# The MLP's seven half-block products over the prompt's tokens only, with the sample's tokens on the stationary side

## The chip, the cores and the metric

The kernel runs on one core of one Trainium2 chip. The metric is the device time of one execution in microseconds; lower is better. A profiled execution has its own time, and a span from its first to its last instruction. TensorE appears as PE (matmuls) and PEld (loads of the stationary side), VectorE as DVE, ScalarE as ACT, GpSimd as POOL and SyncE as SP. SP and POOL here mostly issue DMAs.

## The reference

The model has two layers over 1024 tokens of a prompt and 8 × 16 = 128 tokens of a sample, with 1024 features, all in fp32. Only the MLP of each layer is changed:

```python
def sq_relu_mlp(h, w_up, w_down):
    return jnp.square(jax.nn.relu(h @ w_up)) @ w_down
...
xp = xp + sq_relu_mlp(rmsnorm(xp, norm_ffn[layer]), w_up[layer], w_down[layer])
xs = xs + sq_relu_mlp(rmsnorm(xs, norm_ffn[layer]), w_up[layer], w_down[layer])
```

`w_up` is 1024 × 4096 and `w_down` 4096 × 1024, so a layer's MLP has 32 chunks of 128 hidden rows (`NF`). After layer 1 a final RMSNorm gives the outputs for both kinds of token.

## The kernel before, in words

Features lie on the 128 partitions and the tokens are columns: 1152 of them (`T`), the sample's 128 last. A matrix product keeps fp32 precision by splitting each operand into a high and a low fp32r part, and runs three matmuls, hi·hi, hi·lo and lo·hi (`SPLIT`). In a matmul the weights are stationary (128 × 128) and the tokens move (128 × n columns).

`rest(layer, ...)` does the second half of a layer: the output projection, the MLP, and the start of what follows. Its MLP uses a seven-product scheme on 2 × 2 blocks, in place of eight. The blocks of the tokens are two halves of the features by two halves of the 1152 columns (`TW` = 576 each). A product over 576 columns is two matmuls of 288 (`TQ`).

**Up.** As the output projection's chunks arrive, `evac` adds them to the residual, and `combine(c)` forms the seven combinations of the normed tokens (`b11`, `t2`, `t1`, `b21`, `t3`, `b22`, `t4`), each split into hi and lo; eleven steps for each of four feature chunks c. A unit `unit(m)` (16 a layer) then makes two chunks of hidden rows. `raw(m)` loads its weights, `two_sums` and `seven(i)` form and split the seven weight combinations, two products ahead of their use, into six buffers that take turns. `mms` (line 1525) runs the 12 matmuls of a product for one column quarter, and `take`/`done` sum the products from PSUM, apply the token's RMSNorm factor, ReLU (L1532) and square (L1533), and form the combinations that the down product needs. POOL's queue writes these to DRAM (`hb_d`). The first unit begins with the feature chunks 0 to 2 of its first three products, while `combine(3)` still runs, and then does chunk 3.

**Down.** `todos` lists 7 products × 16 items (`j`, two chunks of hidden rows each); in layer 1 the last product, 5, runs its column halves `n` one after the other. For an item, SP loads the tokens' combination (`load_b`) and the weights (`load_w`, `resident`); ACT and DVE split them (`split_b`, `weights_hi` L1693, `weights_lo` L1699), two to three items ahead; `products` (L1750) runs 12 matmuls for each column quarter. `run_at(i)` holds what is issued ahead of item i. The first two of these, `begin(0)` and `begin(1)`, are issued inside the last unit, before its products 5 and 6. When a chain of products ends, DVE adds the PSUM banks to the residual (L1755), and small steps of the next stage (`later`) are put between items: squares, splits for layer 1, the final norm's outputs (L1914).

The work on one engine runs in the order in which it stands in that engine's program. A scheduler may move an instruction ahead of others by its estimate of when it is ready, except the ones issued by `pinned`. An instruction that waits holds up all that stand behind it on its engine.

Of the kernel before, what the change touches and what calls it, by code (L numbers as in the profile page):

```python
# [15 lines left out]
P = 128  # L16
# [17 lines left out]
TW = T // 2  # L34
TQ = T // 4
TF = 96
# [88 lines left out]
def tile_trunk(ctx, tc, ins, outs):  # L125
# [54 lines left out]
    hb_d = [dram.tile([7, NF // 2, P, TW], F32, name=f"hb_d{l}") for l in range(2)]  # L180
# [76 lines left out]
    def rstd_of(r, pl, acc, scale, eps, name, pin=lambda ins: ins, tp=P):  # L257

        ms = bank(f"ms_{name}")
        for j in range(NG):
            ins = mm(ms[:tp, j:j + 1], acc[:, j * tp:(j + 1) * tp], ones[:, 0:1], start=True, stop=True)
            if j == 0:
                pin(ins)
        v = pl.tile([P, 2, NG], F32, tag="rv", name=f"v_{name}")
        m, y = v[:tp, 0], v[:tp, 1]
        nc.vector.tensor_scalar(m, ms[:tp, 0:NG], scale, eps, ALU.mult, ALU.add)
# [9 lines left out]
        def diag(dg):  # L278
            box["dg"] = dg[:tp, :NG * tp]
            for j in range(NG):  # L280
                nc.vector.tensor_scalar_mul(dg[:tp, j * tp:(j + 1) * tp], ident[:tp, :tp], y[:, j:j + 1])

        def rows():
            ps = bank(f"rr_{name}")
            pin(mm(ps[:, :NG * tp], ones[:tp], box["dg"], start=True, stop=True))
            ACT(r, ps[:, :NG * tp], AF.Copy)
# [1053 lines left out]
    def rest(layer, ks, cat, rst, mp, then, soon=None):  # L1340
# [17 lines left out]
        spare = [own(f"xr{n}", F32) for n in range(4)]  # L1358
        few = [own(f"hl{n}", F32R, 1024) for n in range(2)]
        third = own("th", F32R)  # L1360
        temps = [own(f"tm{n}", F32) for n in range(2)]
# [9 lines left out]
        combos = {k: pair(slots[n], T) for n, k in enumerate(there)}  # L1371
        combos.update({(key, 2): pair(low[n], T) for n, key in enumerate(("t1", "b21", "t3"))})

        def combo(key, c):

            if (key, c) not in combos:
                combos[key, c] = pair(place(*where[key, c], F32R, f"{key}{name}"), T)
            return combos[key, c]
# [22 lines left out]
        def combine(c):  # L1401
# [3 lines left out]
            one, two = slice(0, TW), slice(TW, T)  # L1405
            d, t3, t2, t4 = (t[:, h] for t in temps for h in (one, two))

            def halves(key, src, w):
                hi, lo = (combo(key, c)[:, i] for i in range(2))
                if w is None:  # L1410
                    split(hi, lo, src)
                else:
# [13 lines left out]
                    lambda: halves("t4", t4, None)]  # L1426

        def evac(n, ps, g):
# [4 lines left out]
            if g == NG - 1:  # L1433
                put(xr_d[layer][fc], x[fc])
                if n % 2:
                    todo.extend(combine(fc - 4))

                    todo.append((lambda: (old(n + 3), old(n + 4))) if n < 4 else (lambda: raw(n // 2 - 2)))
            some(3)
            if n == KC - 1 and g == 1:  # L1440
                seven(0)


        raws, ups, parts = {}, {}, [0]
        pinned = tc.keep_in_program_order

        def raw(m):

            if m < NF // 2 and m not in raws:
                raws[m] = [spare[m % 2 * 2 + e][:, :1024] for e in range(2)]  # L1450
                for e in range(2):
                    dma(raws[m][e], ins["w_up"][layer, 2 * m + e])

        def two_sums(m, pin=lambda ins: ins):
            a11, a21, a22 = raws[m][0][:, :512], raws[m][1][:, :512], raws[m][1][:, 512:]
            s1 = ups["s1"] = sp.tile([P, 512], F32, "st", f"s1{name}{m}")
# [4 lines left out]
        def seven(i):  # L1461

            if i in ups or i >= 7 * NF // 2:
                return
            m, k = divmod(i, 7)
            a1, a2 = raws[m]
            a11, a12, a21, a22 = a1[:, :512], a1[:, 512:], a2[:, :512], a2[:, 512:]
            if k == 0:
                src = a11
            elif k == 1:  # L1470
                if "s1" not in ups:
                    two_sums(m)
                src = a11
            elif k == 2:
                src = ups.pop("s1")
# [11 lines left out]
            if k == 0 and m:  # L1487
                pinned(ACT(w[:, 0], src, AF.Copy))
                pinned(tt(w[:, 1], src, f(w[:, 0]), ALU.subtract))
            else:  # L1490
                split(w[:, 0], w[:, 1], src)
            ups[i] = w

        works = [("b11", 0), ("t2", 1), ("t1", 2), ("b21", 0), ("t3", 1), ("b22", 2), ("t4", 1)]
        hids = []
        tmps = [temps[n // 4][:, n % 4 * TQ:n % 4 * TQ + TQ] for n in range(8)]

        t3, t2 = extra[:, :TW], extra[:, TW:]

        def last_sum(m):  # L1500

            pinned(tt(t3, hids[m % 2 * 2 + 1][:, :TW], t2, ALU.subtract))
            put(hb_d[layer][6, m], t3)

        def unit(m):

            if m:
                raw(m + 1)
            if m == 0:
                hids.extend([own("th", F32), *(place(c, i, F32, f"hd{name}") for c, i in ((5, 1), (6, 0), (6, 1)))])  # L1510
            hd = [hids[m % 2 * 2 + e] for e in range(2)]
            banks, tmp = {}, {}

            def to(e, half, n):

                return hd[e][:, half * TW + n * TQ:half * TW + n * TQ + TQ]

            def mms(k, n, ks):
                key, b = works[k]
                if (b, n) not in banks:  # L1520
                    banks[b, n] = bank(f"u{name}{m}{b}{n}")
                w = ups[7 * m + k]
                for c in ks:
                    for i, (a, h) in enumerate(SPLIT):
# [506 lines left out]
```

## Time and profile before

| what | value |
|---|---|
| median of 3 runs | 2714.48 us (2708.94 to 2715.2) |
| time of the profiled execution | 2718.14 us |
| its span | 2716.3 us |
| mean granted TensorE clock | 0.993 of full speed |
| DVE / ACT busy | 2039.7 / 1364.3 us |
| MLP of layer 0: up, down | 580.8 to 946.7 us, 946.7 to 1307.1 us |
| MLP of layer 1: up, down | 1975.4 to 2342.4 us, 2342.4 to about 2704.7 us |

The profiled execution's time is 1.8 us over its span. The two MLPs, four stretches of some 360 us, take a little over half of the span. A matmul's duration in a trace includes its way through the array, so the cost of one in a stream is read from the distance between starts. In a timeline row stand the start, the duration of the whole run of equal instructions, the engine, the line, the operation, output<-inputs, the shape and the count; a bracket gives the idle time before and what ended it. Idle time of DVE, ACT or a queue costs nothing unless PE waits for it.

### The profile page before, as it was taken

To read this page: it belongs to the slowest core of one execution; us is meant where nothing else is said; L and a number is where in the kernel's file an instruction comes from. 1 tells how busy PE (TensorE), PEld (TensorE's weight loads), DVE (VectorE), ACT (ScalarE), POOL (GpSimd) and SP (SyncE) were. 2 spreads that over 40 slices of the span, in tenths; PEclk is the share of its full clock that TensorE was granted. 3 is DMA by queue.
4 is the path that set the end of the run, shared out by engine and by line. 5 is a ranking of instruction groups with operands and counts; after the bars stand their busy time and mean duration, and the time that the engine had idled before them with its cause. 6 is when DMAs were issued, how large, how long until landed. Compare 5 with 4: busy or idle time off the path is not lost.

```text
span 2716.3 us, 50519 instructions
## 1 busy us (share of the span) xinstructions
PE 2661.6 (98%) x19362; PEld 2552.7 (94%) x19362; DVE 2039.7 (75%) x4105; ACT 1364.3 (50%) x2854; POOL 331.1 (12%) x599
## 2 busy tenths in 40 slices
PE   8999999999999999999999999999999999999998
PEld 8888877899999999999999999988999999999998
DVE  8999986887777755768577777778787777647587
ACT  6344456755555533445355555556555555534344
POOL 1100111131111100000011111110321111100001
PEclk9999999999999999999999999999999999999999
DMA  4344547543333486335444444446533333674344
GB/s 159 109 125 149 151 152 232 173 143 139 139 139 142 150 283 228 110 108 185 142 135 136 141 138 139 134 142 226 177 136 142 143 139 148 234 259 132 97 122 146
DMA packets 173203, 422.90 MB, mean 156 GB/s; under 512 B 25968, under 2 KB 53808, under 8 KB 170912
## 3 DMA queue, kind: packets, MB, share of 16 engines
q1 hardware_dynamic: 135696, 288.38, 32.6%
q0 software_dynamic: 37120, 131.27, 14.0%
q8 instruction: 152, 2.49, 0.4%
q14 instruction: 91, 0.75, 0.1%
q10 hardware_dynamic: 144, 0.02, 0.0%
HBM read 289.60 MB, written 117.34 MB: 150 GB/s over the span
## 4 chain that ended last, share of the span: by engine, by line
PE 84%; DVE 8%; DMA 3%; ACT 3%; issue 2%; SPq 0%; POOL 0%; DVEq 0%; ACTq 0%; POOLq 0%
PE pd L1750 26%; PE um L1525 25%; PE psc L225 10%; PE psp L225 4%; PE psoa L225 2%; PE avc L486 2%; PE tpc L474 2%; PE f L225 1%; PE ava L415 1%; PE zs L587 1%; DVE y L754 1%; PE zc L1261 1%; PE so L621 1%; PE psg L225 1%; PE psa L225 1%
## 5 line engine op out<-in xcount | busy, mean ns | idle before, releaser
L225 PE MATMUL psc<-h,hl_wc 128*128 128x384 f32 x1728 | 329.4, 340 | 0.0
L225 PEld LDWEIGHTS psc<-h,hl_wc 128*128 128x128 f32 x1728 | 297.3, 188 | 9.2 <-issue 7.9
L1525 PE MATMUL um<-sl,hl_m 128*128 128x288 f32 x1548 | 240.5, 296 | 0.0
L1525 PEld LDWEIGHTS um<-sl,hl_m 128*128 128x128 f32 x1548 | 218.0, 189 | 0.0
L1750 PE MATMUL pd<-tm,hl_wd 128*128 128x288 f32 x1584 | 214.7, 294 | 0.0
L1750 PEld LDWEIGHTS pd<-tm,hl_wd 128*128 128x128 f32 x1584 | 211.3, 189 | 0.0
L754 DVE SCALAR_TENSOR_TENSOR y<-u,dw,y 128x1024 f32<-128x1024 f32 (+1 forms) x232 | 177.6, 806 | 0.7
L1532 ACT ACTIVATE hdm<-hdm 128x288 f32<-128x288 f32 x192 | 84.7, 442 | 156.4 <-DVE hdm L1531 154.6
L225 PE MATMUL psp<-h,hl_wi 128*128 128x384 f32 x864 | 162.4, 340 | 0.0
L186 DVE TENSOR_TENSOR tm<-xr,tm 128x576 fp32r<-128x576 f32 (+1 forms) x120 | 85.7, 715 | 93.6 <-ACT tm L185 93.3
L225 PEld LDWEIGHTS psp<-h,hl_wi 128*128 128x128 f32 x864 | 148.3, 188 | 6.2 <-issue 5.1
L185 ACT ACTIVATE tm<-xr 128x576 fp32r<-128x576 f32 (+1 forms) x120 | 77.6, 646 | 94.8 <-PE pd L1750 76.2
L1525 PE MATMUL um<-sl,hl 128*128 128x288 f32 x756 | 119.1, 296 | 0.0
L1750 PE MATMUL pd<-th,hl_wd 128*128 128x288 f32 x792 | 113.5, 296 | 3.8 <-DVE th L186 3.6
L1750 PE MATMUL pd<-xr,hl_wd 128*128 128x288 f32 x792 | 112.6, 296 | 0.0
L1750 PEld LDWEIGHTS pd<-th,hl_wd 128*128 128x128 f32 x792 | 108.0, 190 | 4.7 <-DVE th L186 4.1
L1228 ACT ACTIVATE s<-s,mxc 128x640 f32<-128x640 f32 (+4 forms) x128 | 88.8, 694 | 40.0 <-DVE mxc L1225 38.2
L1750 PEld LDWEIGHTS pd<-xr,hl_wd 128*128 128x128 f32 x792 | 108.2, 190 | 0.0
L1525 PEld LDWEIGHTS um<-sl,hl 128*128 128x128 f32 x756 | 106.4, 188 | 0.8
L1750 PE MATMUL pd<-tm,hl 128*128 128x288 f32 x768 | 104.9, 295 | 0.0
L185 ACT ACTIVATE whc<-tpc 128x512 fp32r<-128x512 f32 (+1 forms) x144 | 72.3, 524 | 63.8 <-PE tpc L474 60.5
L1750 PEld LDWEIGHTS pd<-tm,hl 128*128 128x128 f32 x768 | 103.1, 188 | 0.0
(532 smaller groups left out, 6536.9 us busy)
## 6 DMA issues: line engine op xcount, KB each, us to landing
xr<-hb_d SPq DMA_DIRECT2D x208, 288.0 KB, 2.9
xr<-in_w_up_dram SPq DMA_DIRECT2D x64, 512.0 KB, 4.1
hb_d<-hdm POOLq DMA_DIRECT2D x96, 288.0 KB, 2.4
hb_d<-t POOLq DMA_DIRECT2D x96, 288.0 KB, 2.4
wm<-in_w_down_dram SPq DMA_DIRECT2D x64, 256.0 KB, 3.8
st_wd<-in_w_down_dram SPq DMA_DIRECT2D x64, 256.0 KB, 3.4
st_wc<-in_w_in_c_dram SPq DMA_DIRECT2D x44, 256.0 KB, 2.9
xm_d<-xo POOLq DMA_DIRECT2D x16, 576.0 KB, 3.7
```

The source lines that it names most:

```text
L185: ACT(hi, src, AF.Copy)
L186: return tt(lo, src, f(hi), ALU.subtract)
L225: mm(ps()[:, :G], hl[:, a, at:at + P], act[g][k // 4][b][:, k % 4, :], start=n == 0, stop=n == len(todo) - 1)
L415: mm(st["av"][64 * m:64 * m + 64, o0:o0 + n], vs[:, j, i], st["w"][gi][:, c0:c0 + n], start=gi == 0, stop=gi == last)
L474: nc.tensor.transpose(tp[:, c0 + q * P:c0 + (q + 1) * P], blocks.get(j, tile_q), ident)
L486: mm(st["av"][:, o0:o0 + n], vs[:, j, i].rearrange("p a d -> p (a d)"), src[:, c0:c0 + n], start=st["done"] == 0, stop=st["done"] == nmm - 1)
L587: mm(box["z"][at // 512][own, at % 512:at % 512 + kw], qb[:, own], k[:, b * kw:b * kw + kw], start=True, stop=True)
L754: stt(src if j == CW - 1 else dst, src, wj, dst, ALU.mult, ALU.add)
L1228: ACT(s[:, :n], s[:, :n], AF.Exp, bias=mx, scale=-1.0, accum_out=tot)
L1525: mm(banks[b, n][:, :TQ], w[:, a, c * P:c * P + P], combo(key, c)[:, h, n * TQ:n * TQ + TQ], start=k < 3 and c == 0 and i == 0, stop=c == ...
L1532: ACT(y, y, AF.Relu)
L1750: mm(ps, w[:, a, m * P:m * P + P], b[:, h, (n - ns[0]) * TQ:(n - ns[0]) * TQ + TQ], start=first and s == 0, stop=j == NJ - 1 and s == 2, s ...
```

## The change

- The seven products run over the prompt's 1024 tokens alone, in halves of 512 (`TH`). A product is one matmul of 512 columns where two of 288 stood; only layer 1's last product has two halves of 256.
- Two units are merged into one (`units(u)`, 8 a layer), since a product's 512 columns fill a PSUM bank. A product's weights for both (`e` = 0, 1) lie next to each other, in three pairs of buffers that take turns where there were six single ones; `seven(i, e)` still runs two products ahead. The weights of the next pair are loaded when the last use of the ones before has been split, and not a unit earlier.
- The sample's 128 tokens are left out of the seven products. They are the stationary side of four ordinary products (`s1` with weights 0 and 2, `s2` with 3, `sd` with 6), in which the same split weights move: 48 matmuls of 256 columns in a pair of units (L1616), and 192 of 512 columns in a layer's down part (L1909). `combine` gets two more steps for `s1`, `s2`, `sd`.
- The sample's hidden rows come out with tokens on the partitions. `sample_rows` applies the norm factor and ReLU at the start of the next pair, `sample_hidden` turns them with four PE transposes (L1581), squares, splits and writes them to DRAM (`hs_d`). The down part loads them (`load_s`, a further SP load for 128 of the items), and `sample_back` turns each of its three sums with four transposes and adds it to the residual.
- The first pair begins with the chunks 0 to 2 of products (0,0), (1,0), (2,0) and (0,1); the second index is `e`.
- Down takes four PSUM banks a chain, and one for the sample. `last_sum` of the last pair moves from item 3 to item 0. The final norm's last piece is 256 tokens of the prompt, and its outputs come in two blocks of 128 tokens, where there were three of 96.

```diff
-TW = T // 2
-TQ = T // 4
-TF = 96
+TH = 512
+TQ = 256
+NS = slice(TP, T)
...
+        def sample_combo(key, c):
+            return [home(k, c)[:, NS] for k in {"s1": ("b11", "t2"), "s2": ("b21", "b22"), "sd": ("t1", "t3")}[key]]
...
-                    lambda: halves("t4", t4, None)]
+                    lambda: halves("t4", t4, None),
+                    lambda: (halves("s1", x1[:, NS], w1), halves("s2", x2[:, NS], w2),
+                             ACT(sd, x1[:, NS], AF.Copy, scale=w1)),
+                    lambda: (stt(sd, x2[:, NS], w2, sd, ALU.mult, ALU.subtract), halves("sd", sd, None))]
...
-            if i % 6 < 4:
-                w = sp.tile([P, 2, 512], F32R, "hl", f"hl_{name}{i}")
-            else:
-                w = pair(few[i % 6 - 4])
...
+            if i not in ups:
+                if i % 3 < 2:
+                    both = [sp.tile([P, 2, 512], F32R, "hl", f"hl_{name}{i}{a}") for a in range(2)]
...
+                    w = [t.rearrange("p a t -> p (a t)") for t in both]
+                else:
+                    w = few
+                ups[i] = [by_unit(t) for t in w]
...
+            if k > 4:
+                raw(m + 2, k - 5)
...
+        def sample_rows(u):
...
+            ACT(f(at[0]), samples.pop(u)[:, :512], AF.Relu, scale=token_rows["s"])
...
+        def sample_hidden(u):
...
+            for n in range(4):
+                nc.tensor.transpose(tp[:, n * P:n * P + P], f(y)[:, n * P:n * P + P], ident)
...
+            ACT(y, tp[:, :512], AF.Square)
...
-                        mm(banks[b, n][:, :TQ], w[:, a, c * P:c * P + P], combo(key, c)[:, h, n * TQ:n * TQ + TQ],
+                        mm(banks[b, e], w[a][:, c], combo(key, c)[:, h],
...
+            def sample(k):
...
+                        mm(samples[u][:, e * 256:e * 256 + 256], sample_combo(key, c)[h],
+                           w[a][:, c].rearrange("p e t -> p (e t)"), start=k == 0 and c == 0 and i == 0,
...
+                early = ((0, 0), (1, 0), (2, 0), (0, 1))
...
+                if u and k == 0:
+                    last_sum(u - 1)
+                    sample_rows(u - 1)
+                if u and k == 1:
+                    sample_hidden(u - 1)
...
-        at(3, 5, last_sum, NF // 2 - 1)
+        at(0, -1, last_sum, NU - 1)
+        at(0, -1, sample_rows, NU - 1)
+        at(2, 7, sample_hidden, NU - 1)
...
+            for q, (a, h) in enumerate(SPLIT):
+                mm(rows[e], s[:, h], w[:, a], start=j == 0 and q == 0 and k != 0, stop=j == NJ - 1 and q == 2 and k != 3,
+                   skip_group_check=k in (3, 0))
```

How the instructions move shows at two places. The first is PE's program where the up part of layer 0 begins. Before, from the second product's first matmul on (`um` are PSUM banks, `t2m` and `sl`, `lo` the token combinations, `hl_m` the split weights):

```order
L1525 MATMUL um_6309<-t2m_01_5841,hl_m_6272 128x288 [waits Activation_49]
L1525 MATMUL um_6309<-t2m_01_5841,hl_m_6272 128x288
L1525 MATMUL um_6309<-t2m_01_5841,hl_m_6272 128x288 [waits DVE_49]
L1525 MATMUL um_6309<-t2m_11_5998,hl_m_6272 128x288 x3
L1525 MATMUL um_6309<-t2m_21_6145,hl_m_6272 128x288 x3
L1525 MATMUL um_6319<-t2m_01_5841,hl_m_6272 128x288 x3
L1525 MATMUL um_6319<-t2m_11_5998,hl_m_6272 128x288 x3
L1525 MATMUL um_6319<-t2m_21_6145,hl_m_6272 128x288 x3
L1525 MATMUL um_6341<-sl_5644,hl_m_6299 128x288 [waits Activation_49]
```

And now, from the third group's end on; `hl_5633` and `hl_m_6244`, `hl_m_6245` are weights:

```order
L1604 MATMUL um_6350<-sl_5645,hl_5633 128x512 [waits DVE_49]
L1604 MATMUL um_6350<-sl_5646,hl_5632 128x512 x2
L1604 MATMUL um_6350<-sl_5646,hl_5633 128x512
L1604 MATMUL um_6350<-lo_5637,hl_5632 128x512 x2
L1604 MATMUL um_6350<-lo_5637,hl_5633 128x512
L1604 MATMUL um_6368<-b11m_00_5808,hl_m_6244 128x512 [waits Activation_49]
L1604 MATMUL um_6368<-b11m_00_5808,hl_m_6244 128x512
L1604 MATMUL um_6368<-b11m_00_5808,hl_m_6245 128x512 [waits DVE_49]
```

A group is 9 matmuls of 512 columns where there were 18 of 288, and a fourth group, the first product for `e` = 1, has its own weights to wait for.

The second place is ACT's program where up ends and down begins in layer 0. Before (`hdm` are hidden rows, `th` and `xr` the first split tokens of the down part, `hl_wd` its split weights):

```order
L185 ACTIVATE hl_m_10144<-xr_5629 128x512 [waits DVE_49]
L185 ACTIVATE hl_m_10178<-xr_5630 128x512
L185 ACTIVATE th_10272<-xr_10214 128x576 [waits DMAHW1_49,DMASW7_49,DMASW3_49]
L185 ACTIVATE xr_10275<-xr_10214 128x576 [waits DMAHW2_49,DVE_49]
L1532 ACTIVATE hdm_60_6277<-hdm_60_6277 128x288 [waits DMASW4_49,DVE_49]
L1533 ACTIVATE hdm_60_6277<-hdm_60_6277 128x288 [waits Activation_49]
L1693 ACTIVATE hl_wd_10266<-lo_10219 128x512 [waits DMAHW4_49,PE_49]
L1532 ACTIVATE hdm_60_6277<-hdm_60_6277 128x288 [waits DVE_49]
```

Now (`usm` is the sample's PSUM bank, complete with the last matmul of the up part):

```order
L1628 ACTIVATE xr_5630<-xr_5630 128x512 [waits DVE_49]
L1629 ACTIVATE xr_5630<-xr_5630 128x512 [waits Activation_49]
L1573 ACTIVATE sl_9079<-usm_8770,v_m_6411 128x512 [waits PE_49]
L186 ACTIVATE th_9024<-xr_8964 128x512 [waits DMAHW1_49,DMASW0_49,DVE_49]
L1628 ACTIVATE hdm_51_6424<-hdm_51_6424 128x512 [waits DVE_49]
L1629 ACTIVATE hdm_51_6424<-hdm_51_6424 128x512 [waits Activation_49]
L1830 ACTIVATE hl_wd_9018<-lo_8968 128x512 [waits DMAHW4_49]
```

The first tokens and weights of the down part are now split behind the sample's ReLU (L1573), which waits for PE's last matmul of the up part; before, they stood four and more hidden-row steps ahead of that end.

More of the change, by code (lines that the diff above doesn't have):

```diff
@@ new lines, in seven @@
+            if i == 1:
+                hl = pair(third) if e == 0 else ups["spare"]
+                parts = [hl[:, a].rearrange("p (c t) -> p c t", c=4) for a in range(2)]
+            else:
+                parts = [w[:, :, e] for w in ups[i]]
+            src = src.rearrange("p (c t) -> p c t", c=4)
+            if k == 0 and u:
+                pinned(ACT(parts[0], src, AF.Copy))
+                pinned(tt(parts[1], src, f(parts[0]), ALU.subtract))
+            else:
+                split(parts[0], parts[1], src)
@@ L1494, in rest @@
+            ups[i, e] = parts
+            if k > 4:
+                raw(m + 2, k - 5)
         works = [("b11", 0), ("t2", 1), ("t1", 2), ("b21", 0), ("t3", 1), ("b22", 2), ("t4", 1)]
[L1495 to L1518, printed above, removed]
+        sample_works = {0: ("s1", 0), 3: ("s2", 0), 2: ("s1", 1), 6: ("sd", 1)}
@@ new lines, in rest, with hid, t2, put_pair @@
+        hids = {}
+        NU = NF // 4
+        token_rows = {}
+        samples = {}
+        def hid(e, half):
+            if (e, half) not in hids:
+                hids[e, half] = {(0, 0): lambda: own("th", F32), (1, 0): lambda: place(5, 1, F32, f"hd{name}"),
+                                 (0, 1): lambda: spare[2], (1, 1): lambda: spare[3]}[e, half]()[:, :1024]
+            return hids[e, half]
+        t3 = extra[:, :1024]
+        def t2():
+            return nx.sums[:, :1024]
+        def put_pair(k, u, src):
+            put(hb_d[layer][k, 2 * u:2 * u + 2].rearrange("m p t -> p m t"), src.rearrange("p (m t) -> p m t", m=2))
@@ new lines, in products @@
+            ps = banks[m, n][:, :b.shape[2]]
+            for s, (a, h) in enumerate(SPLIT):
+                mm(ps, w[:, a, m * P:m * P + P], b[:, h], start=first and s == 0, stop=j == NJ - 1 and s == 2,
+                   skip_group_check=k not in heads)
+            if j == NJ - 1:
+                for e, half in out[k]:
+                    at = half * TH + (n or 0) * TQ
+                    xs = x[4 * e + m][:, at:at + b.shape[2]]
+                    pinned(tt(xs, xs, ps, ALU.add))
+        rows = {}
@@ new lines, in sample_back @@
+        def sample_back(k):
+            e = sums[k][0]
+            tp = bank(f"pt{layer}{k}")
+            for m in range(4):
+                nc.tensor.transpose(tp[:, m * P:m * P + P], extra[:, 512 + m * P:512 + m * P + P], ident)
+            for m in range(4):
+                xs = x[4 * e + m][:, NS]
+                tt(xs, xs, tp[:, m * P:m * P + P], ALU.add)
+            if k != 6:
+                later.extend(then(x, e, 2, None, sq))
+        order_of = [chain_k for chain in chains for chain_k in chain]
@@ L1872, in then0 @@
             splits = [lambda c=c: n1.split(x[c][:, cols], c, cols) for c in cs]
-            if half == 0:
+            if half == 2 and e == 1:
+                return squares + splits
+            if half != 1:
                 early.extend(splits)
```

391 lines of the change are left out of this document (236 added, 155 removed).

## The prediction

> **What bounds the kernel now.** I read the page first: busy shares, then the chain that ended last, by engine and by line.
>
> ```profile
> span 2716.3 us, 50519 instructions
> PE 2661.6 (98%) x19362; PEld 2552.7 (94%) x19362; DVE 2039.7 (75%) x4105; ACT 1364.3 (50%) x2854; POOL 331.1 (12%) x599
> PE 84%; DVE 8%; DMA 3%; ACT 3%; issue 2%; SPq 0%; POOL 0%; DVEq 0%; ACTq 0%; POOLq 0%
> PE pd L1750 26%; PE um L1525 25%; PE psc L225 10%; PE psp L225 4%; PE psoa L225 2%; PE avc L486 2%; PE tpc L474 2%; PE f L225 1%; PE ava L415 1%; PE zs L587 1%; DVE y L754 1%; PE zc L1261 1%; PE so L621 1%; PE psg L225 1%; PE psa L225 1%
> ```
>
> PE is busy nearly throughout, and the two MLP lines alone make 51% of the chain. Inside the MLPs the question is whether anything else holds PE up. PE's waits in layer 0's MLP, then in layer 1's (columns: total us, times, longest):
>
> ```profile
> PE pd L1750 <- DVE th L186: 1.9, 1, 1.9
> PE um L1525 <- ACT hl_m L185: 1.2, 1, 1.2
> PE um L1525 <- DVE hl_m L186: 0.7, 1, 0.7
> ...
> PE um L1525 <- ACT hl_m L185: 1.7, 1, 1.7
> PE pd L1750 <- DVE th L186: 1.7, 1, 1.7
> ```
>
> Each of these happened once, at the up part's start (`hl_m`) or at its handover to down (`th`). Between these places PE never waits. So the change is worth what it does to PE's stream, plus what it does at these seams; DVE's and ACT's work counts only where it becomes late.
>
> **PE's stream.** Layer 0's down part in PE's timeline, its start and the first instruction behind it:
>
> ```profile
> 946.68 1.10 PE L1750 MATMUL pd<-th,hl_wd 128*128 128x288 f32 x7
> 949.70 2.65 PE L1750 MATMUL pd<-th,hl_wd 128*128 128x288 f32 x13 [1.93 <-DVE th L186]
> ...
> 1307.12 0.72 PE L263 MATMUL ms_h<-ones,acch 128*128 128x1 f32 x6
> ```
>
> The part has 7 x 16 x 24 = 2688 matmuls, and 2681 of them begin from 949.70 on: 357.42 / 2681 = 133.3 ns for 288 columns. For 512 columns the nearest is a stretch of attention, and for 256 two single places:
>
> ```profile
> 500.98 0.39 PE L960 MATMUL z<-k,q 128*128 128x512 f32 x1
> 501.21 0.40 PE L961 MATMUL z<-l,q 128*128 128x512 f32 x1
> 501.44 0.40 PE L960 MATMUL z<-k,q 128*128 128x512 f32 x1
> 501.68 0.39 PE L961 MATMUL z<-l,q 128*128 128x512 f32 x1
> 501.90 0.22 PE L963 MATMUL z<-maskd,unit 128*128 128x128 f32 x1
> ...
> 369.54 0.28 PE L961 MATMUL z<-l,q 128*128 128x256 f32 x1
> 369.66 0.23 PE L963 MATMUL z<-maskd,unit 128*128 128x128 f32 x1
> ...
> 2697.79 1.74 PE L1750 MATMUL pd<-th,wkm 128*128 128x288 f32 x12
> 2699.37 0.60 PE L1921 MATMUL yt<-ident,sl 128*96 128x128 f32 x4
> 2699.72 0.65 PE L1750 MATMUL pd<-xr,wkm 128*128 128x288 f32 x3
> ```
>
> From start to start, four of 512 columns take 0.92 us, 230 ns each; with starts rounded to 0.01 us the ends are 227.5 and 232.5. One of 256 takes 0.12 us, of which I take 118 ns: the line through 288 at 133.3 and 512 at 230 gives 119.5. Four transposes take 0.35 us.
>
> Counts come from the code. A pair of units has 7 x 2 x 12 = 168 matmuls of 512 columns and 48 of the sample with 256, so 16 pairs have 2688 and 768. A layer's down part has 7 x 16 x 12 = 1344 of 512, but in layer 1 product 5 is 16 x 24 of 256: 2496 and 384 in all. The sample's down products are 192 of 512 a layer, 384. In sum 5568 of 512 columns and 768 + 384 = 1152 of 256. Transposes: 64 for the hidden rows and 24 for the sums, 22 groups of four.
>
> - before: 2 x 5376 x 133.3 ns = 1433.2 us
> - after: 5568 x 230 ns = 1280.6, 1152 x 118 ns = 135.9, 22 x 0.35 = 7.7, together 1424.2 us
>
> That is **-9.0 us**; the ends of the 512 column price alone make it -22.9 and +4.9. The columns that pass through the array do not fall: 10752 x 288 = 3.097 million before, 5568 x 512 + 1152 x 256 = 3.146 million now. All of the gain is that fewer matmuls have fewer fixed parts.
>
> The Trainium skill ("TensorE: Matmul & The Clock Gate", section "Back-to-back issue gap") gives two prices for a warm matmul: an isolated gap of N/2.4 + 2.5 ns, and for a stream of load and matmul about 131 ns at N = 512. By the first, an estimate, 288, 512 and 256 columns would cost 122.5, 215.8 and 109.2 ns, and the matmuls would go from 1317.1 to 1327.4 us, a loss of 10.3. By the second, 512 columns would be as cheap as 288 are here, 730 us in place of 1280.6. The trace agrees with neither: 133.3 ns and 230 ns are what stands in it.
>
> **The seams.** Layer 0's up part begins so, PE first, then DVE and ACT on the second product's weights:
>
> ```profile
> 580.77 2.56 PE L1525 MATMUL um<-b11m,hl_m 128*128 128x288 f32 x18
> 584.51 0.53 PE L1525 MATMUL um<-t2m,hl_m 128*128 128x288 f32 x2 [1.19 <-ACT hl_m L185]
> 585.71 3.75 PE L1525 MATMUL um<-t2m,hl_m 128*128 128x288 f32 x16 [0.67 <-DVE hl_m L186]
> ...
> 583.10 0.69 DVE L1459 TENSOR_TENSOR xr<-s1m,xr 128x512 f32<-128x512 f32 x1
> 583.83 0.63 ACT L185 ACTIVATE hl_m<-xr 128x512 fp32r<-128x512 f32 x1 [3.19 <-DVE xr L1459]
> ```
>
> PE has run 18 matmuls, 2.4 us, when it waits 1.2 us for a sum that DVE made at 583.10, and 0.7 us for the low part. Now a group is 9 x 230 ns = 2.1 us, so the cover of these sums is 0.3 us less. The fourth group needs the sums of `e` = 1, a further set that didn't stand ahead of it before, made on DVE between `combine(3)`'s steps, with the high copy on ACT behind that step's own copies. I estimate these weights some 2 us late (a sum and two splits, 0.69 + 0.63 + 0.69, less slack I can't see). With the shorter cover: **+2.5 us a layer, +5 in all**, ends 0 and +10. If DVE fits the sums into its gaps, it is the lower end.
>
> The handover to down, ACT's and DVE's rows around layer 0's last up matmul:
>
> ```profile
> 931.00 0.67 ACT L185 ACTIVATE th<-xr 128x576 fp32r<-128x576 f32 x1
> ...
> 937.28 0.63 ACT L1693 ACTIVATE hl_wd<-lo 128x512 fp32r<-128x512 f32 x1 [0.18 <-PE um L1525]
> ...
> 948.23 0.75 DVE L1539 TENSOR_TENSOR hdm<-hdm 128x576 f32<-128x576 f32 x1
> 948.90 0.75 DVE L186 TENSOR_TENSOR th<-xr,th 128x576 fp32r<-128x576 f32 x1
> ```
>
> The high copies were made 16 and 9 us before down began at 946.68; only the low part of `th` came late, behind DVE's last hidden rows, and cost 1.9 us. Now the sample's ReLU stands ahead of both high copies on ACT, and it waits for PE's last up matmul. Behind it ACT runs the ReLU, `th` high, two steps of hidden rows and `hl_wd` high: five passes of 512 columns, at 0.63 us each (the row at 583.83) about 3.1 us, plus some 0.4 us for the last matmul to drain (0.39 us of duration, row 501.68). PE stands 3.5 us instead of 1.9 and 1.7: **+3.4 us in all**, ends 0 (were the order on ACT not the order by time) and +6. The sample's transposes wait for ACT too, but they stand seven steps into item 2, over 5 us later.
>
> **DVE in down.** Three rows of DVE in layer 1, an operation of 576 columns and two of 512:
>
> ```profile
> 2605.51 0.75 DVE L1838 TENSOR_TENSOR accfin<-accfin,t 128x576 f32<-128x576 f32 x1
> 2606.18 0.68 DVE L1679 TENSOR_TENSOR wm<-wm,lo 128x512 f32<-128x512 f32 x1
> 2606.78 0.68 DVE L1674 TENSOR_TENSOR st_wd<-st_wd,lo 128x512 f32<-128x512 f32 x1
> ```
>
> They follow at 0.67 and 0.60 us, so DVE's token work gets a tenth cheaper, and an item's PE time goes from 24 x 133.3 = 3.2 to 12 x 230 = 2.8 us, or 3.5 with the sample's three. DVE and PE shrink together; I take layer 0's busiest product, 5, with its weight sums and later steps at **+0.5 us** (0 to 2).
>
> In layer 1 product 5 runs its halves one after the other, and the weights of all 16 items must be kept during the first:
>
> ```profile
> 2674.42 0.69 DVE L1699 TENSOR_TENSOR wkm<-st_wd,wkm 128x512 fp32r<-128x512 f32 x1
> 2674.61 3.32 PE L1750 MATMUL pd<-tm,wkm 128*128 128x288 f32 x24
> ```
>
> The last item's weights are ready at 2675.1, and PE reaches it 12 matmuls into the second row, at 2676.2: 1.1 us of slack. This half goes from 16 x 12 x 133.3 = 25.6 us to 16 x 12 x 118 = 22.7 us, 2.9 us shorter, and DVE's chain is the same number of operations. Of the 2.9 us gained (they stand in PE's term) I give back **+1.5** (0 to 4).
>
> **Transfers.** The 128 further loads (`hs_d`) go into SP's queue ahead of the tokens' ones; one landed in
>
> ```profile
> xr<-hb_d SPq DMA_DIRECT2D x208, 288.0 KB, 2.9
> ```
>
> 2.9 us, and they are issued two to three items ahead, over 5.5 us. At nothing, then; without that lead an item would wait some 3 us.
>
> **The tail.** DVE's part of the last outputs:
>
> ```profile
> 2708.60 2.06 DVE L1945 TENSOR_SCALAR yo<-yt,v_fin 96x512 f32<-96x512 f32 x3
> ```
>
> Three blocks of 0.69 us become two, the final sums and squares are over 256 columns instead of 288, and four output DMAs follow rather than six: **-1.5 us** (-2.5 to 0).
>
> **The sum.** -9.0 + 5 + 3.4 + 0.5 + 1.5 - 1.5 = -0.1 us against the profiled 2718.14 us, which is 3.7 over the median of the runs, 2714.48 us. Carried to the median: 2714.4, so I say **2714 us**. A difference within 0.3%, 8.1 us, is about what a measurement of this kernel can tell from no change; faster is below 2706.3, slower above 2722.6.
>
> **Rivals.**
>
> *Forecast, no change (chance 0.40):* the fixed cost saved in the stream is given back at the seams. For it: both seams have the waiting engine shown above. Its own range is 2706 to 2722.
>
> *A, the seams stay as they are (0.30):* 512 columns in a long stream come at the low end, 227.5 ns, since the price here is from four matmuls between others. Then PE's term is -22.9, the seams +5 in all and the tail -1.5: -19, 2695; with 230 ns and seams at nothing, -9.0 - 1.5 gives 2704. The middle is 2700. For it: DVE is at 75% and ACT at 50%, so there is room. Against it: the order on ACT at the handover.
>
> *B, the weights of a pair become late (0.17):* this one is slower. At each pair's start DVE makes three sums of 1024 columns where a unit had three of 512. From the 0.07 us that 64 columns cost, a sum of 1024 takes 0.60 + 8 x 0.07 = 1.16, so three take 1.7 us longer; the lead of two products falls from 2 x 3.2 to 2 x 2.76 us, 0.9 less. DVE loses 2.6 us of its lead at every pair, just ahead of the sums of the next product. No wait there in the trace of before says that the lead was enough, not by how much; I reckon with some 2 us or more, and it decides from 2.6 us down. If it falls short by 1 to 1.5 us at 14 boundaries (7 in each layer), it costs 14 to 21 us: 2732 in the middle.
>
> *C, columns alone set the price (0.05):* 133.3 ns / 288 is 0.463 ns a column, 512 would cost 237.0 and 256 118.5 ns. After is then 5568 x 0.2370 + 1152 x 0.1185 + 7.7 = 1463.8 us, +30.6, and with the seams at their sum 2754. Against it stand the four gaps of 230 ns; if the weight loads of the MLP slow the stream further than attention's, it could come partly.
>
> *D, DVE binds in down (0.08):* product 5 at its upper ends in both layers (+6) with the seams at theirs (+16): -9.0 + 6 + 16 - 1.5 = +11.5, 2726. For it: 1.1 us of slack in layer 1.
>
> **How the numbers follow.** Faster has A's 0.30 and the part of the forecast's own spread below 2706 (0.02): 0.32. Slower has B, C and D, 0.30, of which 0.02 may end within the bound: 0.28. The same: 0.40. The range leaves out A's far end below 2699 (0.08) and above 2735 a third of B, and C (0.11 together): 2699 to 2735.
>
> **What would show it.** PE's stream in layer 0's down part: 12 matmuls every 2.76 us; 2.85 would speak for C, 2.73 for A. PE's waits in layer 0's MLP: the largest at the fourth early group for ACT's or DVE's `hl_m`, and at L1889 for `hl_wd` or `th`, about 3.5 us. Repeated waits at L1604, some 14 in all, for weights of the next pair would show B. Layer 1's product 5 with waits for `wkm` would show D. My forecast is wrong if the MLPs' four stretches together change by more than 8 us, and its working is wrong, even at the right time, if the seams show no longer waits.

## The result and the profile after

| | before | after |
|---|---|---|
| median | 2714.84 us (2708.94 to 2716.74, 4 runs) | 2737.48 us (2734.41 to 2738.82, 4 runs) |
| ratio | | 1.0078, 95% interval 1.0066 to 1.009 |
| profiled execution | 2718.14 us | 2734.41 us |

The change makes the kernel slower by 0.8%, about 22 us. The page of the kernel after has the same shape as that of before:

```profile
span 2732.6 us, 42141 instructions
...
PE 2672.6 (98%) x15404; PEld 2317.0 (85%) x15404; DVE 1988.5 (73%) x3820; ACT 1342.6 (49%) x2691; POOL 314.8 (12%) x535
```

PE has 3958 matmuls fewer and is busy 11 us longer. PE's waits in layer 0's MLP and then in layer 1's, with the tail (total us, times, longest), and below them three of before in layer 1 that the prediction didn't show:

```profile
PE pd060None L1889 <- ACT hl_wd L1830: 4.0, 1, 4.0
PE um L1604 <- ACT hl_m L186: 2.8, 1, 2.8
PE ps L1909 <- DMA sm<-hs_d: 0.8, 1, 0.8
PE um L1604 <- ACT th L186: 0.7, 1, 0.7
PE pd060None L1889 <- DVE hl_wd L1836: 0.3, 1, 0.3
PE um L1604 <- DVE hl L187: 0.3, 1, 0.3
...
PE pd160None L1889 <- ACT hl_wd L1830: 4.5, 1, 4.5
PE um L1604 <- ACT hl_m L186: 2.8, 1, 2.8
PE ms_fin L265 <- DVE accfin L2008: 2.2, 1, 2.2
PE rr_fin L287 <- DVE accfin L283: 1.1, 1, 1.1
PE um L1604 <- DVE hl_m L187: 0.6, 1, 0.6
PE pd L1889 <- DVE wkm L1836: 0.4, 1, 0.4
PE um L1604 <- DVE hl L187: 0.3, 1, 0.3
```

```profile
PE um L1525 <- DVE t2m L186: 0.9, 1, 0.9
PE um L1525 <- DVE hl_m L186: 0.7, 1, 0.7
PE um L1525 <- ACT t2m L185: 0.3, 1, 0.3
```

The waits stand at the two seams, the fourth early group (`hl_m`) and the handover (`hl_wd`), once a layer each, with smaller ones beside them. No wait repeats from pair to pair, so the sums of a pair's weights are in time.

**The stream between the seams.** The hidden rows' transposes stand once in each pair of units, at the same place. The first and the last of seven in layer 0:

```profile
643.81 0.60 PE L1581 MATMUL utm<-ident,tm 128*128 128x128 f32 x4
...
914.04 0.60 PE L1581 MATMUL utm<-ident,tm 128*128 128x128 f32 x4
```

Six pairs take 270.23 us, 45.04 us each. In the kernel before, the last matmuls of a unit, 13 units apart in layer 1:

```profile
2051.93 0.57 PE L1525 MATMUL um<-t4m,hl_m 128*128 128x288 f32 x3
...
2341.96 0.57 PE L1525 MATMUL um<-t4m,hl_m 128*128 128x288 f32 x3
```

290.03 / 13 = 22.31 us a unit, 44.62 for two: 132.8 ns a matmul. Each pair has become 0.42 us longer, where the prediction's prices make it 0.13 us shorter. In layer 0's down part, from the second item to the first instruction behind it:

```profile
963.52 0.86 PE L1889 MATMUL pd060None<-xr,hl_wd 128*128 128x512 f32 x3
...
1316.59 0.72 PE L265 MATMUL ms_h<-ones,acch 128*128 128x1 f32 x6
```

353.07 us for 111 x 12 + 63 x 3 = 1521 matmuls and three groups of transposes (1.07 us): 231.4 ns, an average of two prices. Two places in layer 1 show them, weights in `hl_wd` first, in `hl` then:

```profile
2369.17 0.86 PE L1889 MATMUL pd162None<-tm,hl_wd 128*128 128x512 f32 x3
2369.87 0.86 PE L1889 MATMUL pd163None<-tm,hl_wd 128*128 128x512 f32 x3
...
2373.33 0.84 PE L1889 MATMUL pd163None<-th,hl 128*128 128x512 f32 x3
2374.01 0.84 PE L1909 MATMUL ps<-hl,xr 128*128 128x512 f32 x3
```

From start to start, 0.70 us for three is 233.3 ns, 0.68 is 226.7. `hl_wd` and `hl_m` hold two of three split weights.

**The clock.** The windows after layer 0's early wait (the third number from the end is the granted clock), and those of before at the same place:

```profile
586.00:588.00 2.00, 0.08 (x1) 0.08 (x1) 2.00 (x5) 1.15 (x2) 0.00 (x0) 0.84 0.28 111
588.00:590.00 2.00, 1.87 (x4) 1.06 (x5) 2.00 (x5) 0.63 (x1) 0.00 (x0) 0.50 0.00 0
...
598.00:600.00 2.00, 2.00 (x6) 1.61 (x5) 0.88 (x2) 1.97 (x5) 0.00 (x0) 0.50 0.00 0
600.00:602.00 2.00, 2.00 (x11) 1.67 (x11) 2.00 (x15) 0.66 (x3) 0.00 (x0) 0.75 0.00 0
```

```profile
586.00:588.00 2.00, 2.00 (x11) 2.00 (x11) 2.00 (x4) 2.00 (x5) 1.95 (x3) 0.57 0.56 224
588.00:590.00 2.00, 2.00 (x12) 2.00 (x10) 2.00 (x3) 2.00 (x4) 1.40 (x1) 0.57 0.73 295
```

After PE had stood still, it ran at half clock for some 13.6 us here (6.8 us lost, the sum of 2 us x (1 - clock) over the windows), and for 3.4 us in the kernel before (1.7 lost). Summed that way over all MLP seams, 10.2 us are lost after and 5.1 before; one of the before's three pieces began in layer 1 at 1989.2, behind waits of 0.3 and 0.9 us for `t2m`.

**The ledger** of the two profiled executions, which are 16.3 us apart by their spans:

| term | predicted | measured |
|---|---|---|
| PE's stream: up 16 x 0.42, down 0.2 and 2.7 | -9.0 | +9.6 |
| waits at the early groups: 3.7 and 3.7 after, 1.9 and 3.6 before | +5 | +1.9 |
| waits at the handovers: 5.1 and 4.5 after, 1.9 and 1.7 before | +3.4 | +6.0 |
| half clock at the seams | not in the sum | +5.1 |
| DVE in product 5 (`wkm` 0.4, `rr_fin` 1.1) | +2.0 | +1.5 |
| the tail | -1.5 | -0.5 |
| outside the MLPs | 0 | -7.4 |

The MLP's rows make 24.1 us; its four stretches are 24.2 us longer by their boundaries. (The 2.7 of layer 1's down part is what its stretch has left when its waits and its half-clock time are taken off.) The -7.4 lies in the attention stages, whose code is the same: 5.1 us of it is half-clock time that this execution of the kernel before had there and the one of after had not; the other 2.3 us are not traced to a cause. The medians, 22.6 us apart, hold less of that chance. Each execution's mean granted clock is known, too: 0.990 to 0.993 in the four of the kernel after, 0.991 to 0.996 in the 48 of the kernel before that were taken beside the experiments. Span x (1 - clock) gives, as an estimate, 24 us of lost time after and 17 before on the average. So some 7 of the 22.6 us are half-clock time, of which this pair of executions shows 0.8.

### The profile page after: what moved, and what is told of

It reads as the page before. It is cut to its first block, busy times and chain, and to the rows that moved or that the text cites. A ratio compares the mean times of both kernels' runs of the same rounds, so it can differ in the third digit from the quotient of the medians.

```text
span 2732.6 us, 42141 instructions
## 1 busy us (share of the span) xinstructions
PE 2672.6 (98%) x15404; PEld 2317.0 (85%) x15404; DVE 1988.5 (73%) x3820; ACT 1342.6 (49%) x2691; POOL 314.8 (12%) x535
## 4 chain that ended last, share of the span: by engine, by line
PE 83%; DVE 9%; ACT 3%; DMA 3%; issue 2%; POOL 0%; SPq 0%; DVEq 0%; ACTq 0%; POOLq 0%
PE um L1604 22%; PE psc L226 10%; PE psp L226 4%; PE usm L1616 3%; PE ps L1909 3%; PE psoa L226 2%; PE avc L488 2%; PE tpc L476 2%; PE f L226 1%; PE pd100None L1889 1%; PE pd000None L1889 1%; PE pd001None L1889 1%; PE pd101None L1889 1%; PE pd002None L1889 1%; PE pd102None L1889 1%
## 5 line engine op out<-in xcount | busy, mean ns | idle before, releaser
L1604 PE MATMUL um<-sl,hl_m 128*128 128x512 f32 x780 | 201.9, 398 | 0.0
L1604 PEld LDWEIGHTS um<-sl,hl_m 128*128 128x128 f32 x780 | 145.2, 188 | 34.3
L187 DVE TENSOR_TENSOR tm<-xr,tm 128x512 fp32r<-128x512 f32 (+1 forms) x120 | 78.2, 652 | 101.6 <-ACT tm L186 101.4
L186 ACT ACTIVATE tm<-xr 128x512 fp32r<-128x512 f32 (+1 forms) x120 | 71.9, 599 | 124.0 <-PE pd103None L1889 26.1
L1227 DVE CUSTOM_DVE_ANT_0 s<-zc,bp 128x384 f32<-128x384 f32 (+3 forms) x128 | 66.0, 517 | 41.3 <-PE zc L1264 40.8
L1604 PE MATMUL um<-sl,hl 128*128 128x512 f32 x372 | 94.2, 392 | 0.5 <-DVE hl L187 0.5
L187 DVE TENSOR_TENSOR wlc<-tpc,whc 128x512 fp32r<-128x512 f32 (+1 forms) x144 | 83.1, 594 | 7.5 <-ACT whc L186 6.7
L1604 PE MATMUL um<-b11m,hl_m 128*128 128x512 f32 x288 | 72.5, 404 | 6.3 <-ACT hl_m L186 5.5
L476 PE MATMUL tpc<-ident,s 128*128 128x128 f32 x480 | 73.5, 276 | 3.6 <-DVE s L1232 3.0
L1604 PEld LDWEIGHTS um<-b11m,hl_m 128*128 128x128 f32 x288 | 54.8, 195 | 18.8 <-ACT hl_m L186 6.4
```

The costliest lines, as they stand in the source:

```text
L186: ACT(hi, src, AF.Copy)
L187: return tt(lo, src, f(hi), ALU.subtract)
L476: nc.tensor.transpose(tp[:, c0 + q * P:c0 + (q + 1) * P], blocks.get(j, tile_q), ident)
L1227: nc.vector.tensor_tensor_reduce(s[:, c:c + m], z, b, -1.0, mx, ALU.add, ALU.min, new)
L1604: mm(banks[b, e], w[a][:, c], combo(key, c)[:, h], start=k < 3 and c == 0 and i == 0, stop=c == 3 and i == 2, skip_group_check=k > 2)
```

## The experiments

Each ratio is to the kernel before, on the same chip.

**Start addresses.** The tiles `hl_wd`, `hl_m` start 32 bytes over a multiple of 64 in the built program, `hl` on one. The first experiment shifts all of them, in the kernel after:

```diff
+    const.tile([P, 8], F32, name="pad")
...
+    rst.tile([P, 8], F32, "pad", "pad_rst")
```

> The changed kernel with two unused tiles of 32 bytes, so that the split weights and the token combinations, whose start addresses were 32 over a multiple of 64, lie on a multiple of 64, as the weight pair hl and the tiles th, tm, xr did already. In the changed kernel a 512 column matmul takes 226.7 ns where its weights lie in hl and 233.3 ns where they lie in hl_m or hl_wd. Theory A, the address sets the price: all of them take 226.7 to 228 ns, and with 5568 of them, about 4400 at 233.3 or 231 now, the time falls by 22 to 28 us. Theory B, it is the place in the rotation or what else runs there: 233.3 ns stays for the same weights, and the time stays within 4 us of the changed kernel's 2737.

2731.66 us, ratio 1.006 (1.0045 to 1.0075). `hl_wd` stayed at 230 to 233.3 ns and `hl` at 226.7; a pair took 44.90 us, 0.14 less. The address modulo 64 is not what sets the two prices. The gain in the up parts' stream is some 2 us, and the interval of the ratio overlaps that of the kernel after, so no gain of the whole is shown.

The same edit to the kernel before:

> The kernel before with the same two unused tiles. Its 288 column matmuls take 132 to 133 ns from either kind of address. Theory A in the form that only long matmuls feel the address: within 3 us of the kernel before. Theory A for matmuls of all lengths: 288 columns fall by 3 to 6 ns, and the time by 30 us or more. Theory B: no change.

2715.55 us, ratio 0.9994 (0.9985 to 1.0004): no change that can be told; a unit took 22.26 us, 0.05 less.

**The handover.** First the edit that the prediction's step calls for, the sample's ReLU kept behind the first high copies:

```diff
-            ACT(f(at[0]), samples.pop(u)[:, :512], AF.Relu, scale=token_rows["s"])
+            relu = ACT(f(at[0]), samples.pop(u)[:, :512], AF.Relu, scale=token_rows["s"])
+            if u == NU - 1:
+                pinned(relu)
```

> The changed kernel with the last pair's ReLU of the sample kept in program order on ACT, so that the first high copies of th and hl_wd stand ahead of it. Theory of the prediction, the ReLU's place on ACT makes the handover late: the waits of 4.0 and 4.5 us for hl_wd at the start of the down parts fall below 2.0, the time by some 5 us. Rival, the first weights of the down part lie in the tile lo0, which PE reads until its last sample product (sd), so their load starts only then: the waits stay at 3.5 us or more, and the time within 3 us of 2737.

2738.12 us, ratio 1.0083 (1.0068 to 1.0098). ACT's rows and PE's wait at layer 0's handover:

```profile
953.07 0.63 ACT L186 ACTIVATE th<-xr 128x512 fp32r<-128x512 f32 x1 [4.16 <-DVE xr L1637]
956.47 0.63 ACT L1832 ACTIVATE hl_wd<-lo 128x512 fp32r<-128x512 f32 x1 [1.50 <-DMA lo<-in_w_down_dram]
...
961.35 0.67 ACT L1573 ACTIVATE sl<-usm,v_m 128x512 f32<-128x512 f32 x1
```

```profile
PE pd060None L1891 <- ACT hl_wd L1832: 4.0, 1, 4.0
...
PE pd160None L1891 <- ACT hl_wd L1832: 4.6, 1, 4.6
```

The ReLU (L1573) is 8 us later now, reckoned from PE's first matmul of the down part, and the waits are as they were: 4.0 and 4.6. The step of the prediction falls. What `hl_wd` waits for is its DMA, and `th` waits for DVE's combination that still reads that tile. In the kernel after, PE's last reads of `lo`, SP's load into it, ACT's copy and PE's first matmul stand one behind the other (the timeline, from two engines and SP's queue):

```profile
951.55 0.52 PE L1616 MATMUL usm<-hl_m,lo 128*128 128x256 f32 x3
...
952.11 2.34 SPq L1732 DMA_DIRECT2D lo<-in_w_down_dram  x4
...
955.78 0.63 ACT L1830 ACTIVATE hl_wd<-lo 128x512 fp32r<-128x512 f32 x1 [0.93 <-DMA lo<-in_w_down_dram]
...
956.46 1.22 PE L1889 MATMUL pd060None<-th,hl_wd 128*128 128x512 f32 x2 [4.03 <-ACT hl_wd L1830]
```

The new product `sd` reads `t1` and `t3`, of which chunk 2 lies in the `lo` tiles, as the up part's very last work; the down part's first raw weights go into `lo0`. Before, those tiles were last read in products 2 to 4 of the last unit. So the second edit takes `sd` away from the end:

```diff
+                if u == NU - 1 and k == 6:
+                    sample(6)
                 for n in range(2):
                     mms(k, n)
...
-                sample(k)
+                if not (u == NU - 1 and k == 6):
+                    sample(k)
```

> The changed kernel with the last pair's sample product sd run ahead of the two products of 512 columns at its end, so that PE leaves lo0 and the sample's sums 5.6 us earlier. By the theory of the prediction the ReLU no longer waits for the last matmul, by the rival the weights' load starts 5.6 us earlier: both say that the waits for hl_wd fall from 4.0 and 4.5 us to at most 2, and the time by 4 to 8 us with the clock that stays up. If the waits stay, something else of the last products holds the first weights.

2744.45 us, ratio 1.0105 (1.0088 to 1.0122): not faster but, by the ratios, some 7 us slower than the kernel after, whose interval this one just touches. The waits at the two handovers:

```profile
PE pd060None L1892 <- ACT th L186: 2.0, 1, 2.0
PE pd060None L1892 <- DVE hl_wd L1839: 2.0, 1, 2.0
...
PE pd160None L1892 <- DVE hl_wd L1839: 4.7, 1, 4.7
PE pd160None L1892 <- ACT th L186: 1.5, 1, 1.5
```

The weights were loaded 5 us earlier (SP's row moved from 952.1 to 947.3), but `th` was still DVE's, and the low part of the weights stands behind that of `th` in DVE's program. PE's wait for the high part of `hl_wd` is gone. In layer 1 the two waits together are 6.2 us instead of 4.5, and half clock took 3.6 us more of this execution than of the one with the ReLU behind. The third edit adds to `sd` first that the first items' tokens go into `tm`, which is free by then:

```diff
-                if q < 2:
-                    bsplit.append(pair(own(("th", "xr2")[q], F32R)))
+                if q:
+                    bsplit.extend(pair(own(t, F32R)) for t in ("th", "xr2"))
                 else:
                     bsplit.extend(pair(temp_again()[:, h:h + 1024]) for h in (0, 1024))
```

> The kernel with the last sample product sd ahead of the last two products, and in addition the first two items' tokens split into tm, which is free, in place of th and xr2, which hold hidden rows until DVE's combinations of product 5. In the run with sd first PE still stood 2.0 us for th and 2.0 us for the low part of hl_wd, and 1.5 and 4.7 us in layer 1. If th was what came next, the wait for tokens goes, and at most 2.5 us for hl_wd are left: 4 to 8 us less than with sd first alone, 2737 or less. If DVE's chain of combinations (three of 1024 columns, 1.2 us each) holds the low part of the weights, the waits stay at 3 us or more.

2735.86 us, ratio 1.0068 (1.0049 to 1.0087), by the ratios 10 us less than `sd` first alone, where 4 to 8 were expected: the waits at the handovers are 6.4 us shorter in all, and this execution lost 4.4 us less at half clock.

```profile
PE pd060None L1892 <- DVE th L187: 1.9, 1, 1.9
PE pd160None L1892 <- DVE th L187: 1.9, 1, 1.9
```

PE's only wait behind the handover is 1.9 us in each layer, near the 1.9 and 1.7 of the kernel before. So two tiles held it, one behind the other: `lo0` by `sd`, `th` by the hidden rows. (The `tm` edit without `sd` first was not run.)

**The early groups.** The kernel after with three, as before:

```diff
-                early = ((0, 0), (1, 0), (2, 0), (0, 1))
+                early = ((0, 0), (1, 0), (2, 0))
...
+                mms(0, 1)
+                take(0, 1)
+                seven(3, 1)
                 sample(0)
```

> The changed kernel with three early groups as in the kernel before; the first product for e = 1 runs whole, behind the chunk 3 matmuls. By the prediction's step the fourth group and its weights cost the start some 2.5 us a layer: PE's wait of 2.8 us for hl_m goes, and the time falls by 3 to 5 us, more if the clock stays up. Rival: the end of combine(3) on DVE, whose low part of t2 is done 4.6 us after PE's third group, sets the start whatever PE does in between: then a wait of 4 us or more for t2m takes its place, and the time stays within 3 us of 2737 or gets longer.

2734.36 us, ratio 1.0059 (1.0044 to 1.0075), some 5 us under the kernel after by the ratios, whose intervals overlap. Layer 0's waits at the start, of which those for `t2m` are new:

```profile
PE um L1604 <- ACT t2m L186: 0.9, 1, 0.9
...
PE um L1604 <- DVE t2m L187: 0.3, 1, 0.3
```

The wait of 2.8 us for `hl_m` is gone and 1.2 us for `t2m` have come (1.5 in layer 1). By the trace the prediction's step stands, and the rival, that `combine(3)` holds PE for 4 us anyway, falls.

**Columns and fixed part.** Each matmul of 512 columns in the up parts as two of 256:

```diff
-                        mm(banks[b, e], w[a][:, c], combo(key, c)[:, h],
...
+                        for n in (0, 256):
+                            mm(banks[b, e][:, n:n + 256], w[a][:, c], combo(key, c)[:, h, n:n + 256],
```

> The changed kernel with each 512 column matmul of the up parts issued as two of 256 columns, so the same columns in twice as many matmuls. If a matmul has a fixed part beside its columns (120 ns at 256, 232 at 512 in the changed kernel), the 2688 become 5376, a product's 12 matmuls take 2.88 us instead of 2.79, and the two up parts get 2688 x 8 ns = 20 us longer together. If columns alone set the price: no change, within 4 us of 2737.

2758.7 us, ratio 1.0149 (1.0123 to 1.0175), 19 us over the kernel after by the ratios. The first and last transposes of seven, as above:

```profile
648.93 0.60 PE L1581 MATMUL utm<-ident,tm 128*128 128x128 f32 x4
...
926.71 0.60 PE L1581 MATMUL utm<-ident,tm 128*128 128x128 f32 x4
```

277.78 / 6 = 46.30 us a pair, 1.26 more, 20.2 us over 16 pairs. Twice 168 matmuls of 256 columns cost 7.5 ns more for each pair of them than 168 of 512: there is a fixed part beside the columns, and fewer, longer matmuls save it.

**Where the second price comes from.** The pool of `hl_m` and `hl_wd` laid elsewhere in the low part of SBUF (its line ahead of `hpool`'s):

> The changed kernel with the pool of the split weights laid ahead of the pool of the token combinations in SBUF: hl_m and hl_wd then start at 14176 to 26464 bytes and no longer at 87904 to 100192, at the same place modulo 64; the pair hl and the tokens th, tm, xr stay. If it is the neighbourhood of 87904 to 104288 that makes a 512 column matmul 233.3 ns, these now take another time, 226.7 if they lie well. If all addresses below some 110000 are alike in this, or something else than the address sets it, 233.3 ns stays, and the time is within 3 us of 2737.

2740.38 us, ratio 1.0082 (1.0059 to 1.0104), and `hl_wd` stayed at 233.3 ns at 14176 to 26464 bytes. Next, weights of the fast tile `hl` laid in the low part:

```diff
-                w = pair(few[i % 6 - 4])
+                w = pair(few[i % 6 - 4]) if i > 31 else pair(place(7 - i % 2, 1, F32R, f"few{name}"))
```

> The changed kernel with the ten pairs of weights of each layer's first two down products that lay in the tiles hl (132032 and 136128) laid in two tiles at 67936 and 77152, from the pool of the token combinations. If the part of SBUF decides (the low part, which also holds hl_m and hl_wd, against the part from 113600 on), their matmuls go from 226.7 to 233.3 ns: 20 items of 12 or 15 matmuls, 1.8 us in all. If it is the pool that hl_m and hl_wd come from, or their turn in the rotation, they stay at 226.7 ns. The time is within 4 us of 2737 either way.

2740.19 us, ratio 1.0089 (1.0059 to 1.0118). The moved weights:

```profile
971.73 0.87 PE L1889 MATMUL pd061None<-th,fewm 128*128 128x512 f32 x3
972.44 0.86 PE L1889 MATMUL pd062None<-th,fewm 128*128 128x512 f32 x3
```

From start to start 0.71 us for three, 236.7 ns; over the two products' rows the median is 233.3, where it was 226.7. So in the down parts, whose tokens all lie from 122816 bytes on in the built program, where the weights lie sets the price: below 104288 the higher one, from 127424 on the lower.

It isn't the place of the weights alone, though. In the up parts the tokens `b11m` and `t2m` lie below 44384 bytes, and there the kernel after shows the opposite, weights in `hl` first (high), in `hl_m` then (low), with the same tokens:

```profile
2080.07 5.77 PE L1604 MATMUL um<-b11m,hl 128*128 128x512 f32 x24
...
2125.16 5.61 PE L1604 MATMUL um<-b11m,hl_m 128*128 128x512 f32 x24
```

Here the low weights are the cheaper ones, by 0.16 us in 24 matmuls, 6.7 ns each. Over all matmuls with tokens below 44384 the medians are 227 ns with low weights (486) and 234 with high ones (259). So the lower price comes where weights and tokens both lie low or both high; but with tokens from 44896 to 81248 and low weights the median is 234 again (320), and no run takes the cause further.

**How much of PE's time shows.** The sample's MLP products taken out, but for one matmul in twelve and one in three:

```diff
-                for c in range(4):
-                    for i, (a, h) in enumerate(SPLIT):
+                for c in range(1):
+                    for i, (a, h) in enumerate(SPLIT[:1]):
...
-            for q, (a, h) in enumerate(SPLIT):
+            for q, (a, h) in enumerate(SPLIT[:1]):
```

> The changed kernel without most of the sample's MLP products: of a pair's 48 matmuls of 256 columns 4 are left, of the three of 512 columns of a down item one, so the sample's outputs aren't computed. If PE is what bounds every stretch, the time falls by what they take in its stream: 16 x 44 x 119 ns + 256 x 231 ns = 84 + 59 = 143 us, to about 2595. If DVE or the transfers stand just behind PE, less than 120 us of it shows, with new waits at L1604 or L1889.

2613.65 us, ratio 0.9623 (0.9599 to 0.9647): 127 us less than the 2740.19 of the kernel with the weights moved low, on the same chip. Of the 143 expected, 12 went to more half-clock time (32.4 us in this execution, 20.1 in that one) and 5 to longer waits of PE in the MLPs. Nearly all of PE's time off the stream shows in the end time, so the stream bounds the MLPs.

**Together.** Start addresses, three groups, `sd` first and `tm`:

> The changed kernel with three of the edits at once: start addresses on multiples of 64, three early groups, and sd first with the first tokens in tm. Measured apart they stood 6, 3 and 2 us under the changed kernel's 2738. If their gains are of different places and add up: 2725 to 2729, still 8 to 12 us over the kernel before, since PE's stream itself is no shorter than before. If the stream were not what is left, the seams alone would bring it back to the kernel before: 2720 or less.

2721.44 us, ratio 1.0022 (1.001 to 1.0034), between the two times that were expected. By the ratios it stands 15 us under the kernel after and the single runs 5, 5 and 3; the intervals don't tell 15 from their sum, 13. In the profiled execution no half-clock time was left at layer 0's seams and 3.4 us at layer 1's first, 12.8 us in all, where that of the kernel after had 19.6. To these edits the last one adds weights in the upper part of SBUF for all down items (raw weights lie in `hl_wd`'s place):

```diff
...
-            elif i % 6 < 4:
-                w = sp.tile([P, 2, 512], F32R, "hl", f"hl_wd{layer}{i}")
             else:
-                w = pair(few[i % 6 - 4])
+                w = pair(few[i % 6]) if i % 6 < 2 else pair(own(("xr3", "lo1", "lo0", "lo2")[i % 6 - 2], F32R))
```

> The kernel with the three edits together (2721 where the kernel before took 2714.5), and in its down parts the split weights moved from the four tiles hl_wd in the low part of SBUF to four tiles from 122880 on; raw weights lie in hl_wd's place. If the part of SBUF sets a 512 column matmul's price, all matmuls of the down parts take 226.7 ns: about 1850 of them 6.6 ns less, 12 us, and the time is 2705 to 2712, the kernel before or up to 0.4% under it. The raw weights' loads for the first items also no longer wait for the tile lo0. If the price in the few-low run came from something else than the part of SBUF, the rows stay at 232 to 233 ns and the time at 2721; if the raw weights' new places make the loads late, new waits for the weights stand at the products, 2725 or more.

2714.21 us, ratio 0.9988 (0.9979 to 0.9997); the kernel before took 2716.43 us on this chip, so the ratio is as expected, though the time in us is not. Rows of its down part, where one item ends and the next begins:

```profile
1002.29 0.84 PE L1913 MATMUL ps<-hl,xr 128*128 128x512 f32 x3
1002.97 0.84 PE L1893 MATMUL pd060None<-th,xr 128*128 128x512 f32 x3
```

The 512 column matmuls of the down parts take 226.7 ns now (their median is 227). By the ratios that is 9 us, where the price gave 12; PE still waits 2.7 and 3.1 us for `th` behind the handovers. The changed kernel, mended in four places, is level with the kernel before, or 0.1% under it.

## Why the prediction was wrong

It forecast no change, 2714 us with a range of 2699 to 2735; the kernel was slower, 2.5 us beyond the range.

- **PE's stream, the step that failed.** The prediction took -9.0 us, with ends of -22.9 and +4.9; measured +9.6. The mechanism is right (two matmuls of 256 cost more than one of 512, as the halves showed), its size is off by 18.6 us, in three parts. Before was priced at 133.3 ns from a stretch whose start ran at half clock (950 to 956, 1.7 us): without it that stretch gives 132.7, over the four stretches it is about 132.6, and 10752 x 0.7 ns are 7.5 us. After was priced at 230 ns from four matmuls of attention; in the MLP it is 231.4 to 232.2, since more than half of its matmuls have their weights low and their tokens high in SBUF or the other way, at 233 to 234 ns: some 9 us on 5568. And 256 columns take 119 to 120 ns, not 118, 2 us on 1152. Each error is below 1.5%; on a term that is the difference of two sums of 1430 us, they decide its sign. The test that the prediction set itself shows the miss: the four MLP stretches changed by 24.2 us, not by less than 8.
- **Where the saving went.** By measured prices the prompt's matmuls after take 5184 x 231.6 + 384 x 120 ns = 1247 us, and before, at 8/9 of 10752 x 132.6 ns, 1267: 20 us saved. The sample's take 768 x 119 + 384 x 231.4 ns and 22 x 0.35 us, 188 us, where its ninth of the columns took 158. Without the seven-product scheme the sample needs 8/7 of the work, and the transposes: 30 us lost.
- **The early groups.** The place was right, the fourth group's `hl_m` on ACT behind `combine(3)`'s copies, and the three-group run shows it to be the cause. The waits grew by 1.9 us, not 5: by 1.8 in layer 0 and 0.1 in layer 1, which had 3.6 us of them before; the prediction had shown 1.7 of those.
- **The handover.** The forecast wait of 3.5 us was near the 4.0 and 4.5 by luck (with the smaller waits +6.0 us for +3.4), since the reason was wrong: not the ReLU's place on ACT but tiles held by their last readers. The order of an engine shows who stands behind whom; it doesn't show which buffer a new last reader keeps.
- **The clock** stood in the table (0.993 in the mean) and was no term of the sum: 5.1 us at the seams of the profiled pair, some 7 by the estimate from the mean clocks.
- **Rivals.** B (weights of a pair late) didn't come: no wait repeats. C (columns alone) falls by the halves. A's conditions, 227.5 ns throughout or seams at nothing, didn't come; the down parts reach 226.7 only with all weights laid high. D (product 5 at +6 us) didn't come; DVE cost PE 1.5 us there, near the sum's own 2.0.

## What to carry over

Where a change replaces one long stream by another, price both from the same stage and the same buffers, take stalls and slow-clock time out of the stretch, and count the work that leaves a cheaper scheme, before trusting a small difference. A reader added at the end of a stage holds its buffers: ask what is loaded into them next. And a wait removed at a seam shows the next one, so edits there are worth judging together.

## What the runs showed of the hardware

- The place of both operands in SBUF moved the price of a 512 column fp32r matmul. With tokens from 122816 bytes on it took 226.7 ns with weights from 127424 on and 233.3 with weights below 104288; with tokens below 44384 it was 227 with the low weights and 234 with the high ones. With 288 columns no such step was seen: 133.1 ns with high weights and 132.1 with low ones in the down parts before. Why is open; the address modulo 64 isn't it.
- Half-clock time came in pieces of 3.4 us (1.7 lost), singly or up to four in a row, in the MLPs after waits from 0.9 us (layer 1 before, the clock 0.50 from 1990 to 1992) to 4.5 us. It isn't decided by the wait alone: after 2.8 us in layer 0 it lasted 13.6 us, after the same wait in layer 1 of the same execution there was none. The Trainium skill ("TensorE: Matmul & The Clock Gate", section "What's actually happening") gives a free-running window of 3413 ns, which fits the length of the pieces and the chance in them; its idle window of about 3.4 us as the condition does not fit the 1.9 us of layer 0's handover before, after which the clock was 0.50.
